# RWKV-7 pair preparation: decay and in-context rate as one 512-wide chain, biases inside the low-rank matmul

## The chip, the cores and the metric

The kernel runs on one core of one Trainium2 chip. The time is device microseconds (us) from launch to end; before the change it is 2669.53 us, the median of three runs (2666.68 to 2670.61). Engines are named as in the profile: PE (TensorE matmul), PEld (its weight loads), DVE (VectorE), ACT (ScalarE), POOL (GpSimd), SP (the queue from which nearly all DMAs are issued).

## The reference

A two-layer trunk on 256 tokens of width 2048. Layer 0 is RWKV-7 time mixing, layer 1 chunked band attention; each is followed by a squared-ReLU MLP, and every sub-layer has an RMS norm with shift, scale and gate computed from a conditioning vector `c`. The change touches only two lines of layer 0, the decay and the in-context rate:

```python
    w_log = -jax.nn.softplus(-(w0 + jnp.tanh(xw @ w1) @ w2)) - 0.5
    a = jax.nn.sigmoid(a0 + (xa @ a1) @ a2)
...
    decay = jnp.exp(-jnp.exp(heads(w_log)))
```

`w1`, `a1` are 2048x96 and `w2`, `a2` are 96x2048; `w0`, `a0` are bias vectors of 2048. Both lines come down to the same thing: with z the biased low-rank product, exp(w_log) is sigmoid(z) times exp(-0.5), and a is sigmoid(z). The kernel gets a sigmoid as exp(-ln(1 + exp(-z))), so that only exponential and logarithm are needed.

## The kernel before, in words

Everything is kept transposed: 128 channels on partitions, 256 tokens along the free axis. Two heads of 64 channels make a *pair*, and layer 0 has 16 pairs.

`layer_a` first computes, for all pairs, the value projection `v` and the low-rank inner products `tw` (96x256, after tanh, line 830), `ta` (96x256, line 831) and `tg`. Then a loop over slots works through the pairs as a software pipeline. Eight slots belong to one pair's dense projections of k and r (`proj_steps`, 2 x 16 contraction tiles, each as three matmuls: lines 407 to 409). A pair itself is a generator of 36 steps, one per slot: 8 of `early` (decay, rate, normalised key, the operands of the chunked recurrence), 12 of `invert` (a triangular inverse in 32x32 tiles), 16 of `late` (the recurrence over four chunks, group norm, gate). Pair j+1 starts 8 slots after pair j, so that four to five pairs are under way at once, each at its own step. In every slot the PE instructions stand in a fixed order (`issue_after`): the inverting pairs first, then the late ones, then the early one, then two portions of the dense projection. From the third pair on, up to six steps per eight slots of the conditioning product (`ada`, line 460 on DVE, fed by 512 KB loads `raw<-w_ada`) go in as filler. On DVE, ACT, POOL and SP no order is written out: when the program is built, a list scheduler with cost estimates lays their instructions into one queue per engine, and on the chip each queue runs strictly in that order.

The steps at issue, all in `Pair.early`:

- step 0: two fp32 matmuls (lines 133, 134) put w and a side by side into one PSUM bank `z`; then for each half DVE adds the bias column and takes the lower bound -80 (line 138, reads PSUM) and ACT takes exp(-z) (line 140).
- step 1: the square of k for the head norm (lines 121 to 125), then on ACT ln(1+x) for each half (line 144), and exp for each half (lines 145, 146).
- step 2: DVE scans the decay along the tokens (line 151), ACT makes its exponentials (lines 153, 155).
- step 3: DVE clamps the head sums out of PSUM (line 160), ACT takes their rsqrt (161 to 163), POOL computes a-1 times `k_a` (165) and a times e2 (167).

Lines 324 to 332, called below the gate of the oldest pair, are the last `late` steps: ln and exp on ACT, three DVE instructions, and the gate matmul (line 330), whose PSUM bank (tag `ms`, two banks) is the one that line 160 of the youngest pair has just read out. The temporaries `s` are 128x256 tiles from one ring of 8 buffers, the oldest free buffer first; a pair takes 14 of them (among them `sw` and `a`). The low-rank weights of a pair, `lw`, are one DMA on SP (line 864) into a single buffer.

Of the kernel before, what the change touches and what calls it, by code (L numbers as in the profile page):

```python
# [12 lines left out]
F32 = mybir.dt.float32  # L13
F32R = mybir.dt.float32r
AF = mybir.ActivationFunctionType
ALU = mybir.AluOpType
AX = mybir.AxisListType

P = 128
# [13 lines left out]

VECS = ["g_mix0", "g_mix1", "g_mlp0", "g_mlp1", "g_kv", "g_final",
        "mu0", "mu1", "mu2", "mu3", "mu4", "mu5",
        "w0", "a0", "k_k", "k_a", "r_k", "ln_w", "ln_b"]
VI = {n: i for i, n in enumerate(VECS)}


# [38 lines left out]
class Pair:  # L78
# [10 lines left out]
        self.b, self.j, self.v, self.tw, self.ta, self.tg, self.e01 = body, j, v, tw, ta, tg, e01  # L89
        self.heads, self.done = (slice(0, C), slice(C, P)), False  # L90

    def s(self, name="s", bufs=8):
        return self.b.pw.tile([P, T], F32, tag=name, bufs=bufs, name=name)

    def big(self, name, bufs):
# [31 lines left out]

    def early(self):
        b, nc, j, k, r, v, s, ch = self.b, self.b.nc, self.j, self.k, self.r, self.v, self.s, self.ch
        pw, vec, cst, e01 = b.pw, b.vec, b.cst, self.e01  # L130
        lw = self.lw
        z = b.psm()
        nc.tensor.matmul(z[:, 0:T], lw[:, 0, :], self.tw, start=True, stop=True)
        nc.tensor.matmul(z[:, T:2 * T], lw[:, 1, :], self.ta, start=True, stop=True)

        sw, a = s(), s()
        for o, at, b0 in ((sw, 0, "w0"), (a, T, "a0")):
            nc.vector.tensor_scalar(out=o, in0=z[:, at:at + T], scalar1=vec(b0, j), scalar2=-80.0,
                                    op0=ALU.add, op1=ALU.max)
            nc.scalar.activation(o, o, AF.Exp, scale=-1.0)  # L140
        yield
        sq = self.parts(k, None, AF.Square, vec("k_k", j))
        for o in (sw, a):
            nc.scalar.activation(o, o, AF.Ln, bias=b.col(C_ONE))
        nc.scalar.activation(sw, sw, AF.Exp, scale=-1.0, bias=b.col(C_MHALF))
        nc.scalar.activation(a, a, AF.Exp, scale=-1.0)
        yield
        pss = b.psm()[:, :T]
        self.head_sums(pss, sq)
        cum = s()  # L150
        nc.vector.tensor_tensor_scan(out=cum, data0=cst("reset"), data1=sw, initial=0.0, op0=ALU.mult, op1=ALU.add)
        e0, e1 = e01[:, :, 0:C], e01[:, :, 1:C + 1]
        nc.scalar.activation(e1, ch(cum), AF.Exp, scale=-1.0)
        e2 = s()
        nc.scalar.activation(e2, cum, AF.Exp)
        self.pc = pw.tile([P, 4, 1], F32, tag="pc", bufs=4, name="pc")
        nc.gpsimd.tensor_copy(self.pc, e01[:, :, C:C + 1])
        yield
        rs, ss, rr = s(), s(), s()
        nc.vector.tensor_scalar(out=ss, in0=pss, scalar1=1e-24, scalar2=None, op0=ALU.max)  # L160
        nc.scalar.activation(rs, ss, AF.Ln)
        nc.scalar.activation(rs, rs, AF.Exp, scale=-0.5)
        nc.scalar.activation(rr, rs, AF.Square)
        km = s()
        nc.gpsimd.tensor_scalar(out=km, in0=a, scalar1=-1.0, scalar2=vec("k_a", j), op0=ALU.add, op1=ALU.mult)
        self.bh, self.kh = s("bh", 2), s("kh", 2)
        nc.gpsimd.tensor_tensor(out=self.bh, in0=a, in1=e2, op=ALU.mult)
        yield
        nc.vector.scalar_tensor_tensor(out=rr, in0=rr, scalar=-0.5, in1=ss, op0=ALU.mult, op1=ALU.mult)
        nc.vector.scalar_tensor_tensor(out=rs, in0=rr, scalar=1.5, in1=rs, op0=ALU.add, op1=ALU.mult)  # L170
        kk = s()
        nc.vector.scalar_tensor_tensor(out=kk, in0=k, scalar=vec("k_k", j), in1=rs, op0=ALU.mult, op1=ALU.mult)
        nc.vector.scalar_tensor_tensor(out=km, in0=km, scalar=1.0, in1=k, op0=ALU.add, op1=ALU.mult)
        yield
        kr = self.kr = self.big("kr", 4)
        nc.vector.tensor_tensor(out=kr[:, :, 0:C], in0=ch(kk), in1=e0, op=ALU.mult)
        nc.vector.tensor_tensor(out=self.bh, in0=self.bh, in1=kk, op=ALU.mult)
        nc.vector.tensor_tensor(out=kr[:, :, C:P], in0=ch(r), in1=e1, op=ALU.mult)
        rkp = s()
        nc.vector.scalar_tensor_tensor(out=rkp, in0=r, scalar=vec("r_k", j), in1=km, op0=ALU.mult, op1=ALU.mult)  # L180
        nc.vector.tensor_tensor(out=self.kh, in0=km, in1=e2, op=ALU.mult)
        rkp = self.parts(rkp, rkp)
        yield

        self.vp = pw.tile([P, 4, C], F32, tag="vp", bufs=4, name="vp")
        pt = b.psm().rearrange("p (a c k) -> p a c k", a=2, c=4)
        self.each(lambda c: pt[:, 0, c, :], lambda c: ch(v)[:, c, :], lambda c: cst("cen"))
        nc.scalar.copy(self.vp, pt[:, 0])
        yield
        pbn = b.psm()[:, :T]  # L190
        self.head_sums(pbn, rkp)
        nc.vector.tensor_tensor(out=v, in0=pbn, in1=v, op=ALU.mult)
        yield
# [142 lines left out]
class Body:  # L336
# [15 lines left out]
    def vec(self, name, kt=None):  # L352
        i = VI[name]
        return self.vecs[:, i, :] if kt is None else self.vecs[:, i, kt:kt + 1]
# [285 lines left out]
    def layer_a(self, st, sp):  # L640
        nc, tc, d = self.nc, self.tc, self.d
        pa = st.enter_context(tc.tile_pool(name="pa", bufs=1))
        v = pa.tile([P, KT, T], F32, name="v")
        tw = pa.tile([96, T], F32, name="tw")
        ta = pa.tile([96, T], F32, name="ta")
        tg = pa.tile([P, 2, T], F32, name="tg")
        with ExitStack() as s1:
            pp = s1.enter_context(tc.tile_pool(name="ps_a", bufs=2, space=bass.MemoryType.PSUM))
# [178 lines left out]
            self.wnext = self.weight(next(weights))  # L827
            for i in range(4):
                nc.scalar.copy(v[:, 2 * i:2 * i + 2, :], pv[i])
            nc.scalar.activation(tw, pl[0][:96, 0, :], AF.Tanh)  # L830
            nc.scalar.copy(ta, pl[0][:96, 1, :])
            ins = nc.scalar.activation(tg, pl[1], AF.Sigmoid)
            with tc.issue_after(ins.ins):
                nc.scalar.preload_act_table_set("natural_log_exp_and_others")
# [4 lines left out]
        with ExitStack() as s1:  # L839
# [14 lines left out]
            def proj_steps(pr):  # L854
                for dst, hl in (("k", xk), ("r", xr)):
# [4 lines left out]
                    for kt in range(KT):  # L860
                        self.proj(ps, w, lambda kt: hl[:, kt, :, 0:T], (kt, kt + 1))
                        if dst == "r" and kt == 1:
                            pr.lw = pw.tile([96, 2, P], F32, tag="lw", bufs=1, name="lw")
                            nc.sync.dma_start(out=pr.lw, in_=d["lora2"][pr.j, :96, 0:2])
                        if kt % 2 == 1:
                            if kt == KT - 1:
                                t = pw.tile([P, T], F32, tag=dst, bufs=2, name=dst)
                                nc.scalar.copy(t, ps)
                                setattr(pr, dst, t)
                            yield  # L870
# [300 lines left out]
def _arrange(x, c, w_ada, b_ada, g_mix, g_mlp, w_up, w_down,  # L1171
# [7 lines left out]
    x, mu = f(x), f(rwkv_mu)[0]  # L1179
    g_mix, g_mlp = f(g_mix), f(g_mlp)  # L1180
    vecs = [g_mix[0], g_mix[1], g_mlp[0], g_mlp[1], f(g_kv), f(g_final)] + [mu[i] for i in range(6)] + [
        f(rwkv_w0)[0], f(rwkv_a0)[0], f(rwkv_k_k)[0], f(rwkv_k_a)[0], f(rwkv_r_k)[0].reshape(D),
        f(rwkv_ln_w)[0], f(rwkv_ln_b)[0]]

    lora1 = np.concatenate([f(w)[0] for w in (rwkv_w1, rwkv_a1, rwkv_g1)], 1)
    lora1 = f(lora1.reshape(4, 4, P, lora1.shape[1]).transpose(0, 2, 1, 3))
    lora2 = np.zeros((NPAIR, P, 4, P), np.float32)
    for i, w in ((0, rwkv_w2), (1, rwkv_a2)):
        w = f(w)[0]
        lora2[:, :w.shape[0], i, :] = w.reshape(w.shape[0], NPAIR, P).transpose(1, 0, 2)  # L1190
    g2 = f(rwkv_g2)[0].reshape(2, P, NPAIR, P)
    lora2[:, :, 2:4, :] = g2.transpose(2, 1, 0, 3)
# [47 lines left out]
```

## Time and profile before

| | |
|---|---|
| runs, median (lowest, highest) | 2669.53 us (2666.68, 2670.61) |
| the profiled execution: its time, its span | 2667.25 us, 2665.3 us |
| HBM read, mean rate | 656.72 MB, 247 GB/s |
| pairs' first low-rank matmul (line 133), first and last | 213.7 us, 626.4 us |

The profiled execution lies within the three runs. A span is the time from the first to the last instruction; the two microseconds between it and the execution's time lie around it. In the views of the profile, `L138 DVE TENSOR_SCALAR s<-ms,vecs` means that line 138 ran on DVE, writing tile `s` from tiles `ms` and `vecs`; behind `x` stands the number of instances, then their busy time in us and the mean of one in ns. `[0.41 <-DVE s L160]` means that the engine sat idle for 0.41 us just before, until line 160 on DVE released it.

### The profile page before, as it was taken

To read this page: it belongs to the slowest core of one execution; us is meant where nothing else is said; L and a number is where in the kernel's file an instruction comes from. 1 tells how busy PE (TensorE), PEld (TensorE's weight loads), DVE (VectorE), ACT (ScalarE), POOL (GpSimd) and SP (SyncE) were. 2 spreads that over 40 slices of the span, in tenths; PEclk is the share of its full clock that TensorE was granted. 3 is DMA by queue.
4 is the path that set the end of the run, shared out by engine and by line. 5 is a ranking of instruction groups with operands and counts; after the bars stand their busy time and mean duration, and the time that the engine had idled before them with its cause. 6 is when DMAs were issued, how large, how long until landed. Compare 5 with 4: busy or idle time off the path is not lost.

```text
span 2665.3 us, 59286 instructions
## 1 busy us (share of the span) xinstructions
PE 2586.9 (97%) x24108; PEld 2258.5 (85%) x24108; DVE 2104.5 (79%) x3070; ACT 1369.2 (51%) x2516; POOL 210.2 (8%) x336
## 2 busy tenths in 40 slices
PE   7998999999999999999999999999999999999997
PEld 4788888888899888888888998877898888888886
DVE  6788888888889888888888898899887556556555
ACT  3345656556456345355365554565564464553554
POOL 0002323223100000000001100000100000000002
PEclk9999999999999999999999999999999999999999
DMA  9976656566768898889888779887766555555553
GB/s 353 313 243 205 202 183 201 182 202 199 252 235 308 309 324 323 318 328 335 319 328 292 231 248 322 320 274 256 267 215 237 185 188 189 184 188 190 189 190 119
DMA packets 207153, 662.69 MB, mean 249 GB/s; under 512 B 21408, under 2 KB 54560, under 8 KB 206880
## 3 DMA queue, kind: packets, MB, share of 16 engines
q1 hardware_dynamic: 204816, 656.36, 71.8%
q8 instruction: 189, 3.10, 0.5%
q10 hardware_dynamic: 2064, 2.54, 0.3%
q14 instruction: 84, 0.69, 0.1%
HBM read 656.72 MB, written 2.10 MB: 247 GB/s over the span
## 4 chain that ended last, share of the span: by engine, by line
PE 83%; DVE 7%; issue 3%; DMA 3%; ACT 2%; POOL 1%; DVEq 0%; ACTq 0%; SPq 0%; POOLq 0%
PE pj L418 41%; PE pj L419 21%; PE pj L407 3%; PE pj L408 3%; PE pj L409 3%; DVE wL L387 2%; DVE acc L460 2%; DMA raw<-w_ada 1%; PE iv L111 1%; DMA rada<-w_ada 1%; ACT wH L384 1%; PE o L407 1%; PE gr L105 1%; PE ms L330 1%; PE o L408 0%
## 5 line engine op out<-in xcount | busy, mean ns | idle before, releaser
L387 DVE TENSOR_TENSOR wL<-raw,wH 128x1024 fp32r<-128x1024 f32 x772 | 941.1, 1220 | 352.8 <-ACT wH L384 346.9
L384 ACT CAST wH<-raw 128x1024 fp32r<-128x1024 f32 x772 | 805.7, 1045 | 783.6 <-PE pj L418 594.6
L418 PE MATMUL pj<-aHL,wH 128*128 128x512 f32 x2816 | 998.1, 398 | 1.3 <-DVE x L953 1.3
L419 PE MATMUL pj<-aHL,wL 128*128 128x256 f32 x2816 | 791.4, 281 | 0.2 <-DVE wL L387 0.2
L418 PE MATMUL pj<-hHL,wH 128*128 128x512 f32 x2048 | 723.0, 398 | 0.0
L418 PEld LDWEIGHTS pj<-aHL,wH 128*128 128x128 f32 x2816 | 531.6, 189 | 129.4 <-issue 8.5
L419 PE MATMUL pj<-hHL,wL 128*128 128x256 f32 x2048 | 573.8, 280 | 0.3 <-DVE wL L387 0.3
L419 PEld LDWEIGHTS pj<-aHL,wL 128*128 128x128 f32 x2816 | 531.6, 189 | 1.8 <-issue 0.8
L418 PEld LDWEIGHTS pj<-hHL,wH 128*128 128x128 f32 x2048 | 384.7, 188 | 95.0 <-DVE hHL L999 0.2
L419 PEld LDWEIGHTS pj<-hHL,wL 128*128 128x128 f32 x2048 | 386.5, 189 | 0.8 <-DVE wL L387 0.6
L460 DVE SCALAR_TENSOR_TENSOR acc<-rada,ct,acc 128x1024 f32<-128x1024 f32 x256 | 328.2, 1282 | 11.1 <-DMA rada<-w_ada 10.1
L407 PE MATMUL pj<-aHL,wH 128*128 128x256 f32 (+1 forms) x896 | 263.3, 294 | 0.1
L408 PE MATMUL pj<-aHL,wH 128*128 128x256 f32 (+1 forms) x896 | 254.7, 284 | 0.0
L409 PE MATMUL pj<-aHL,wL 128*128 128x256 f32 (+1 forms) x896 | 253.5, 283 | 0.0
L524 POOL TENSOR_TENSOR ss<-ss,sq 128x256 f32<-128x256 f32 x56 | 54.1, 966 | 1588.2 <-ACT sq L523 1587.9
L407 PEld LDWEIGHTS pj<-aHL,wH 128*128 128x128 f32 x896 | 170.5, 190 | 5.1 <-issue 0.5
L409 PEld LDWEIGHTS pj<-aHL,wL 128*128 128x128 f32 x896 | 171.0, 191 | 0.2
L408 PEld LDWEIGHTS pj<-aHL,wH 128*128 128x128 f32 x896 | 170.6, 190 | 0.5
L1024 DVE SCALAR_TENSOR_TENSOR x<-pj,mod,x 128x256 f32<-128x256 f32 x256 | 123.4, 482 | 58.5 <-PE pj L419 54.9
L460 DVE SCALAR_TENSOR_TENSOR acc<-raw,ct,acc 128x1024 f32<-128x1024 f32 x104 | 139.9, 1345 | 12.9 <-DMA raw<-w_ada 12.3
L996 ACT ACTIVATE t<-t 128x256 f32<-128x256 f32 x112 | 46.8, 418 | 123.1 <-DVE t L968 123.1
L998 ACT ACTIVATE t<-t 128x256 f32<-128x256 f32 x128 | 53.4, 417 | 3.4
(250 smaller groups left out, 2825.3 us busy)
## 6 DMA issues: line engine op xcount, KB each, us to landing
raw<-w_up SPq DMA_DIRECT2D x256, 512.0 KB, 4.2
raw<-w_down SPq DMA_DIRECT2D x256, 512.0 KB, 4.3
rada<-w_ada SPq DMA_DIRECT2D x209, 512.0 KB, 5.8
raw<-w_ada SPq DMA_DIRECT2D x111, 512.0 KB, 4.4
rada<-w_ada_kv SPq DMA_DIRECT2D x64, 512.0 KB, 6.1
rawa<-w_ada SPq DMA_DIRECT2D x32, 512.0 KB, 6.8
rawa<-w_ada_t SPq DMA_DIRECT2D x32, 512.0 KB, 7.6
raw<-w_k SPq DMA_DIRECT2D x32, 512.0 KB, 3.9
```

The source lines that it names most:

```text
L384: nc.scalar.copy(Hf, raw)
L387: eng.tensor_tensor(out=Lf, in0=raw, in1=Hf, op=ALU.subtract)
L407: nc.tensor.matmul(ps, H[:, i, :], a(kt)[:, 0, :], start=(first and kt == 0), stop=False)
L408: nc.tensor.matmul(ps, H[:, i, :], a(kt)[:, 1, :], start=False, stop=False)
L409: ins = nc.tensor.matmul(ps, L[:, i, :], a(kt)[:, 0, :], start=False, stop=(last and kt == KT - 1))
L418: nc.tensor.matmul(ps, H[:, i, :], a(kt), start=(kt == 0), stop=False)
L419: ins = nc.tensor.matmul(ps[:, 0, :], L[:, i, :], a(kt)[:, 0, :], start=False, stop=(kt == KT - 1))
L460: nc.vector.scalar_tensor_tensor(out=self.acc, in0=raw, scalar=ck, in1=self.acc, op0=ALU.mult, op1=ALU.add)
L524: (eng or nc.gpsimd).tensor_tensor(out=self.ss, in0=self.ss, in1=sq, op=ALU.add)
L996: nc.scalar.activation(t, t, AF.Relu)
L998: nc.scalar.activation(t, t, AF.Square)
L1024: nc.vector.scalar_tensor_tensor(out=x, in0=ps[:, i, :], scalar=self.mods[(layer, 5)][:, n:n + 1], in1=x, op0=ALU.mult, op1=ALU.add)
```

## The change

The biases become row 96 of the low-rank weights, and the rows 96 to 127 of `tw` and `ta` are set to 1 once (rows 97 to 127 of the weights are zero), so that the matmul adds the bias itself. Then both halves of `z` need the same treatment, and lower bound, exponential and logarithm run over all 512 columns in one instruction each. The two last exponentials stay apart (the decay's has the factor exp(-0.5)). The two halves now live in one double-width tile `s2` with one buffer, and the ring `s` goes from 8 buffers to 6. `w0` and `a0` leave the table `vecs`.

```diff
-    def s(self, name="s", bufs=8):
+    def s(self, name="s", bufs=6):
...
-        sw, a = s(), s()
-        for o, at, b0 in ((sw, 0, "w0"), (a, T, "a0")):
-            nc.vector.tensor_scalar(out=o, in0=z[:, at:at + T], scalar1=vec(b0, j), scalar2=-80.0,
-                                    op0=ALU.add, op1=ALU.max)
-            nc.scalar.activation(o, o, AF.Exp, scale=-1.0)
+        both = pw.tile([P, 2 * T], F32, tag="s2", bufs=1, name="s2")
+        sw, a = both[:, 0:T], both[:, T:2 * T]
+        nc.vector.tensor_scalar(out=both, in0=z, scalar1=-80.0, scalar2=None, op0=ALU.max)
+        nc.scalar.activation(both, both, AF.Exp, scale=-1.0)
         yield
         sq = self.parts(k, None, AF.Square, vec("k_k", j))
-        for o in (sw, a):
-            nc.scalar.activation(o, o, AF.Ln, bias=b.col(C_ONE))
+        nc.scalar.activation(both, both, AF.Ln, bias=b.col(C_ONE))
         nc.scalar.activation(sw, sw, AF.Exp, scale=-1.0, bias=b.col(C_MHALF))
         nc.scalar.activation(a, a, AF.Exp, scale=-1.0)
...
-        tw = pa.tile([96, T], F32, name="tw")
-        ta = pa.tile([96, T], F32, name="ta")
+        tw = pa.tile([P, T], F32, name="tw")
+        ta = pa.tile([P, T], F32, name="ta")
+        for t in (tw, ta):
+            nc.gpsimd.memset(t[96:P, :], 1.0)
...
-            nc.scalar.activation(tw, pl[0][:96, 0, :], AF.Tanh)
-            nc.scalar.copy(ta, pl[0][:96, 1, :])
+            nc.scalar.activation(tw[:96, :], pl[0][:96, 0, :], AF.Tanh)
+            nc.scalar.copy(ta[:96, :], pl[0][:96, 1, :])
...
-                            pr.lw = pw.tile([96, 2, P], F32, tag="lw", bufs=1, name="lw")
-                            nc.sync.dma_start(out=pr.lw, in_=d["lora2"][pr.j, :96, 0:2])
+                            pr.lw = pw.tile([P, 2, P], F32, tag="lw", bufs=1, name="lw")
+                            nc.sync.dma_start(out=pr.lw, in_=d["lora2"][pr.j, :, 0:2])
...
-    for i, w in ((0, rwkv_w2), (1, rwkv_a2)):
-        w = f(w)[0]
+    for i, w, bias in ((0, rwkv_w2, rwkv_w0), (1, rwkv_a2, rwkv_a0)):
+        w = np.concatenate([f(w)[0], f(bias)[0].reshape(1, D)], 0)
```

The rest of the diff takes `w0`, `a0` out of the list `VECS` and out of the array that fills it.

More of the change, by code (lines that the diff above doesn't have):

```diff
@@ L35 @@
         "mu0", "mu1", "mu2", "mu3", "mu4", "mu5",
-        "w0", "a0", "k_k", "k_a", "r_k", "ln_w", "ln_b"]
+        "k_k", "k_a", "r_k", "ln_w", "ln_b"]
 VI = {n: i for i, n in enumerate(VECS)}
@@ L1181, in _arrange @@
     vecs = [g_mix[0], g_mix[1], g_mlp[0], g_mlp[1], f(g_kv), f(g_final)] + [mu[i] for i in range(6)] + [
-        f(rwkv_w0)[0], f(rwkv_a0)[0], f(rwkv_k_k)[0], f(rwkv_k_a)[0], f(rwkv_r_k)[0].reshape(D),
+        f(rwkv_k_k)[0], f(rwkv_k_a)[0], f(rwkv_r_k)[0].reshape(D),
         f(rwkv_ln_w)[0], f(rwkv_ln_b)[0]]
```

## The prediction

> **What bounds the kernel now.** First the page, for the busy shares over the whole span.
>
> ```profile
> PE 2586.9 (97%) x24108; PEld 2258.5 (85%) x24108; DVE 2104.5 (79%) x3070; ACT 1369.2 (51%) x2516; POOL 210.2 (8%) x336
> ```
>
> PE is busy nearly throughout. The changed code runs only while pairs are under way, so I took the windows of that stretch (columns: window, its length, busy us of PE, PEld, DVE, ACT, POOL, the granted clock, DMA share, GB/s).
>
> ```profile
> 213.00:640.00 427.00, 403.63 (x8739) 364.89 (x8737) 362.90 (x660) 252.86 (x711) 120.02 (x179) 0.99 0.62 197
> ```
>
> The clock is full. PE is idle for 427.0 - 403.6 = 23.4 us, DVE for 64 us, ACT for 174 us. A shorter instruction on DVE or ACT is worth something only through PE's 23.4 us. So the next view is who PE's weight loads wait for in this window, and each instance of the wait that the early steps can cause.
>
> ```profile
> PEld ms L330 <- DVE s L160: 4.0, 8, 1.4
> ```
>
> ```profile
> 323.89 0.30 PEld L330 LDWEIGHTS ms<-tg,lg 128*128 128x128 f32 x2 [0.20 <-DVE s L160]
> 380.65 0.30 PEld L330 LDWEIGHTS ms<-tg,lg 128*128 128x128 f32 x2 [0.41 <-DVE s L160]
> 409.70 0.30 PEld L330 LDWEIGHTS ms<-tg,lg 128*128 128x128 f32 x2 [1.42 <-DVE s L160]
> 438.05 0.30 PEld L330 LDWEIGHTS ms<-tg,lg 128*128 128x128 f32 x2 [0.20 <-DVE s L160]
> 467.40 0.30 PEld L330 LDWEIGHTS ms<-tg,lg 128*128 128x128 f32 x2 [0.92 <-DVE s L160]
> 495.61 0.30 PEld L330 LDWEIGHTS ms<-tg,lg 128*128 128x128 f32 x2 [0.26 <-DVE s L160]
> 552.39 0.30 PEld L330 LDWEIGHTS ms<-tg,lg 128*128 128x128 f32 x2 [0.20 <-DVE s L160]
> 609.40 0.30 PEld L330 LDWEIGHTS ms<-tg,lg 128*128 128x128 f32 x2 [0.41 <-DVE s L160]
> ```
>
> The gate matmul of an old pair (L330) wants the PSUM bank that L160 of the young pair has not yet emptied. Eight of these waits, 4.0 us. What lies ahead of L160 shows in the chain of waits between 420 and 450 us (start, us, what), for the pair whose matmul is at 438.05:
>
> ```profile
> 430.65 0.80 DVE s L138 x2
> ...
> 431.45 0.71 ACT s L140 x2
> 432.16 0.80 ACT s L144 x2
> ...
> 434.69 0.36 ACT sl L324
> 435.05 0.94 ACT wH L384
> ...
> 436.02 1.22 DVE wL L387
> ...
> 437.66 0.34 DVE s L160
> ```
>
> The first three links are the instructions that the change merges: 0.80 + 0.71 + 0.80 = 2.31 us of a chain that ends in a PE stall. In the pair before, the same wait has another origin (DVE in order of time):
>
> ```profile
> 398.68 0.88 DVE L138 TENSOR_SCALAR s<-ms,vecs 128x256 f32<-128x256 f32 x2
> ...
> 401.03 1.65 DVE L460 SCALAR_TENSOR_TENSOR acc<-raw,ct,acc 128x1024 f32<-128x1024 f32 x1 [1.48 <-DMA raw<-w_ada]
> ...
> 409.23 0.41 DVE L160 TENSOR_SCALAR s<-ms 128x256 f32<-128x256 f32 x1
> ```
>
> ```profile
> 401.00:409.70 8.70, 7.11 (x172) 6.22 (x167) 8.67 (x14) 6.33 (x18) 7.03 (x9) 1.00 0.80 258
> ```
>
> DVE is done with L138, stands 1.48 us for a load, and from 401.03 works without a gap (8.67 of 8.70 us) until L160 releases PE. Anything saved at 398.68 disappears into the 1.48 us.
>
> **The merged instructions.** Widths and engines have rows in the groups by shape, between 213 and 640 us:
>
> ```profile
> L138 DVE TENSOR_SCALAR s<-ms,vecs 128x256 f32<-128x256 f32 x32 | 14.0, 478 | 2.8 <-PE ms L134 2.4
> L160 DVE TENSOR_SCALAR s<-ms 128x256 f32<-128x256 f32 x16 | 6.6, 412 | 0.1
> L219 DVE TENSOR_TENSOR ar<-gr,csts 128x256 f32<-128x256 f32 x15 | 6.3, 418 | 0.0
> L269 DVE TENSOR_TENSOR mk<-gr,csts 128x512 f32<-128x512 f32 x14 | 9.5, 677 | 0.4 <-PE gr L105 0.2
> ...
> L140 ACT ACTIVATE s<-s 128x256 f32<-128x256 f32 x32 | 11.5, 405 | 0.5 <-DVE s L138 0.3
> L144 ACT ACTIVATE s<-s,csts 128x256 f32<-128x256 f32 x32 | 14.4, 495 | 0.0
> L188 ACT COPY vp<-ms 128x256 f32<-128x256 f32 x15 | 5.6, 373 | 6.4 <-PE ms L105 6.4
> L239 ACT COPY bk<-ms 128x512 f32<-128x512 f32 x15 | 8.8, 587 | 0.6 <-PE ms L105 0.2
> ```
>
> L160 is the new DVE form at half the width: a tensor_scalar from PSUM with constants only, 412 ns; the column operand of L138 made it 478. Doubling a PSUM read costs 677 - 418 = 259 ns, so the new one is an estimated 412 + 259 = 671 ns where the chain has 800: 0.13 us saved. On ACT doubling costs 587 - 373 = 214 ns: exp 405 + 214 = 619 ns against 710, 0.09 us saved; ln 495 + 214 = 709 against 800, 0.09 us. Together 0.31 us per pair as links of a chain. If every removed instruction had cost its full mean it would be (956 - 671) + (810 - 619) + (990 - 709) = 757 ns; that is the far end, but two in a row overlap, as their 0.71 us against 2 x 0.405 shows.
>
> [...]
>
> How much of the 0.31 us reaches PE? The two long waits (1.42 and 0.92) save nothing: the first goes back to the load above, and for the second DVE likewise had to stand for a load:
>
> ```profile
> 460.20 2.08 DVE L460 SCALAR_TENSOR_TENSOR acc<-raw,ct,acc 128x1024 f32<-128x1024 f32 x1 [0.15 <-DMA raw<-w_ada]
> ```
>
> The other six are worth the smaller of the wait and 0.31: 0.20 + 0.31 + 0.20 + 0.26 + 0.20 + 0.31 = 1.48 us. That takes all six to hang on this chain, which I saw for the one at 438.05; the end on the other side is 0. The remaining eight pairs have no such wait and give 0: the dense projection's matmuls hide the early steps, and without that cover they would cost at most 0.31 each, 2.5 us more.
>
> **PE.** The matmuls get 128 rows instead of 96. Both forms have rows (ns min/median/max):
>
> ```profile
> L133 PE MATMUL ms<-tw,lw x32: 377/380/483, 213.9 to 626.6; 96*128 96x256 f32 x32
> ...
> L330 PE MATMUL ms<-tg,lg x64: 377/379/484, 323.9 to 709.1; 128*128 128x256 f32 x64
> ```
>
> 380 against 379 ns: rows cost nothing, the bias addition comes free.
>
> **The loads.** `lw` grows from 96 to 128 KB; a 128-partition load of that size is in the table of DMA issues:
>
> ```profile
> lg<-lora SPq DMA_DIRECT2D x16, 128.0 KB, 2.8
> lw<-lora SPq DMA_DIRECT2D x16, 96.0 KB, 3.9
> ```
>
> It is asked for a whole pair ahead and lands in 3 to 4 us, so its own length is hidden. On SP it stays one issue in the same place. But a `w_ada` load behind it can land later by 32 KB at the window's 197 GB/s, 0.17 us; where DVE already stands for that load and PE for DVE, in two pairs, that is 0.3 us. Bounds: 0 and 16 x 0.17 = 2.7 us. I take 0.3.
>
> **The buffers.** A pair now takes 12 tiles from 6 buffers instead of 14 from 8, so a buffer is wanted again after half a pair. By the code at most five of the tiles are alive at once (e2, rs, ss, rr and km in step 3), and the ring hands out the buffer that has been free longest. The new tile `s2` has one buffer; its last reader is L165 on POOL, and the next pair's writer is L138 at 430.65:
>
> ```profile
> 409.01 0.65 POOL L165 TENSOR_SCALAR s<-s,vecs 128x256 f32<-128x256 f32 x1
> ```
>
> 430.65 - 409.66 = 21 us apart. Neither adds a wait that I can see: 0. Were L165 or L138 to wait after all, POOL's and DVE's queues behind it would wait with it, ada's accumulations first; an upper end for that is the rival below. The two memsets stand on POOL ahead of its first work:
>
> ```profile
> 28.39 2.17 POOL L740 TENSOR_TENSOR xx<-h 128x256 f32<-128x256 f32 x2 [27.94 <-DMA rawa<-w_ada_t]
> ```
>
> 27.94 us of idle time cover them; uncovered they would cost about one L165 each, 1.3 us, once. The shorter `vecs` load is worth nothing that a wait shows.
>
> **The sum.** -1.5 + 0.3 = -1.2 us on the profiled execution's 2667.25, 2666.0. That execution is 2.3 us below the median of the runs; the same difference from 2669.5 gives 2668.
>
> **The rivals.** First, the chain is worth its whole length in every pair, because a stage that saves on DVE and ACT lets PE's other idle time shrink too (23.4 us are there). By the rows in order of time the pair of L138 takes 0.88 us, and the merging saves 0.21 instead of 0.13; the ACT rows are
>
> ```profile
> 400.08 0.72 ACT L140 ACTIVATE s<-s 128x256 f32<-128x256 f32 x2
> ...
> 401.11 0.89 ACT L144 ACTIVATE s<-s,csts 128x256 f32<-128x256 f32 x2
> ```
>
> which gives 0.10 and 0.18: 0.49 per pair, 7.8 us in 16, 2662. For it speaks the chain quoted first, which the three merged links lead; against it the pair at 409.70, where a load stood in between. [...]
>
> Second, slower by DVE's order. DVE's queue is laid out anew by estimates at the build. L160 releases PE, and an accumulation takes
>
> ```profile
> L460 DVE SCALAR_TENSOR_TENSOR acc<-raw,ct,acc 128x1024 f32<-128x1024 f32 x84 | 114.5, 1363 | 12.8 <-DMA raw<-w_ada 12.3
> ```
>
> 1.36 us. Where one more of them comes ahead of L160 or of the scan, PE's wait grows like the one of 1.42 us. In eight pairs: 8 x 1.36 - 1.2 = +9.7 us, 2679; it decides from about five pairs on. For it: the new step is shorter, so there is a hole in the list at that place for a filler to fall into. Against it: the estimates change by few tenths of a microsecond per pair.
>
> Third, the change does nothing for PE at all, everything goes into DVE's standing for loads: 2669.5.
>
> **How the numbers follow.** Forecast 2668 (0.30); full chain 2662 (0.28); DVE's order 2679 (0.27); nothing 2669.5 (0.15). About 0.2%, 5.3 us, is what a measurement of this kernel can tell from no change: forecast and third rival lie inside, which makes 0.45; the first is faster (0.28), the second slower (0.27). The range goes from 2661, just beyond the full chain, to 2678, where seven to eight pairs carry the accumulation; the forecast's own is 2667 to 2670.
>
> **What would show it.** One L138 per pair of about 671 ns, one exp of 619, one ln of 709; the first pair of rows says whether the widths were priced well. PE's waits on L160 fall from 4.0 to about 2.5 us, the two long ones stay. L133 at 380 ns. No idle time before L165 or L138 that a buffer explains. The forecast is wrong if PE's busy time plus idle between 213 and 640 us moves by more than 5 us, and the place to look is then what stands between L151 and L160 in DVE's queue.

## The result, and the profile after

| | before | after |
|---|---|---|
| median of nine runs each (lowest, highest) | 2665.91 us (2662.95, 2673.17) | 2659.24 us (2655.02, 2663.75) |
| profiled execution: time, span | 2667.25, 2665.3 | 2658.25, 2656.5 |

The ratio is 0.9975, 95% interval [0.9965, 0.9985]: faster by 0.25%. The 2659.24 us lie below the predicted range of 2661 to 2678 us. The kernel before lies lower too: the forecast started from 2669.53 us, the median of its first three runs, and nine runs give 2665.91. The experiments below change what the 0.25% means: the same two kernels, run again, were equal.

The changed instructions first (groups by shape of the kernel after, 213 to 640 us; behind the bar busy us, then ns of one):

```profile
L142 ACT ACTIVATE s<-s,csts 128x512 f32<-128x512 f32 x16 | 11.6, 722 | 0.5
...
L138 DVE TENSOR_SCALAR s<-ms 128x512 f32<-128x512 f32 x16 | 11.0, 688 | 1.9 <-PE ms L134 1.6
L139 ACT ACTIVATE s<-s 128x512 f32<-128x512 f32 x16 | 10.1, 630 | 4.6 <-DVE s L138 4.5
```

They are within 3% of the estimates of 671, 619 and 709 ns. L133 is unchanged, at 380 ns with 128 rows (min/median/max), and PE's gate matmul, now L328, waits less for the bank that L158 empties: 3.0 us in three waits, where there were 4.0 in eight.

```profile
L133 PE MATMUL ms<-tw,lw x32: 379/380/483, 213.9 to 624.9; 128*128 128x256 f32 x32
```

```profile
PEld ms L328 <- DVE s L158: 3.0, 3, 1.4
```

```profile
436.02 0.73 PEld L328 LDWEIGHTS ms<-tg,lg 128*128 128x128 f32 x4 [0.87 <-DVE s L158]
465.64 0.51 PEld L328 LDWEIGHTS ms<-tg,lg 128*128 128x128 f32 x3 [1.42 <-DVE s L158]
493.24 0.73 PEld L328 LDWEIGHTS ms<-tg,lg 128*128 128x128 f32 x4 [0.70 <-DVE s L158]
```

So the durations came as estimated, and the sum of the waits came near. The single waits did not: the longest one before (1.42 us at 409.70) is gone with four of the six short ones, and the three left have all grown, from 0.20, 0.92 and 0.26 us at the same pairs. Now the time by stage. The stages are cut at the first, third and sixteenth pair's first L133 (ramp, middle), at the 113th cast of a weight half (tail) and at the 129th, where the output projection is nearly over. Before:

```profile
213.90:261.40 47.50, 39.37 (x546) 35.90 (x545) 37.73 (x59) 24.24 (x55) 11.37 (x13) 0.93 0.68 215
261.40:626.30 364.90, 351.68 (x7905) 318.11 (x7903) 311.96 (x575) 216.85 (x623) 100.84 (x156) 1.00 0.61 193
626.30:712.30 86.00, 79.89 (x1561) 70.27 (x1560) 69.78 (x120) 40.37 (x116) 16.31 (x23) 0.98 0.68 224
...
757.50:2665.30 1907.80, 1890.78 (x12265) 1647.30 (x12263) 1484.88 (x1958) 975.67 (x1534) 56.31 (x111) 1.00 0.74 255
```

After:

```profile
213.90:253.30 39.40, 35.96 (x546) 32.98 (x544) 35.94 (x57) 24.27 (x51) 10.61 (x13) 1.00 0.71 237
253.30:624.60 371.30, 353.98 (x7905) 320.19 (x7903) 307.23 (x562) 215.66 (x597) 103.88 (x156) 0.99 0.60 193
624.60:714.60 90.00, 82.06 (x1561) 71.73 (x1560) 69.81 (x119) 39.90 (x113) 15.00 (x23) 0.94 0.66 214
...
759.10:2656.50 1897.40, 1881.24 (x12265) 1643.63 (x12263) 1481.66 (x1959) 975.66 (x1534) 56.55 (x111) 1.00 0.73 257
```

The number of matmuls is the same in each stage. The ramp is 8.1 us shorter, the middle 6.4 longer, the tail 4.0 longer: pairs 498.4 before, 500.7 after. The 10.4 us gained lie behind 757 us, where no changed instruction runs. Two separate questions follow: what moved the pairs by 8 us each way, and what moved the rest.

**The pairs: idle time and clock.** Length minus PE busy is idle: 8.1 to 3.4 us in the ramp, 13.2 to 17.3 in the middle, 6.1 to 7.9 in the tail. That is 4.7 of 8.1, 4.1 of 6.4 and 1.8 of 4.0 us, about half of each shift or somewhat more. The rest is in PE's busy time itself: the same 546 matmuls of the ramp took 39.4 us at a granted clock of 0.93 and 36.0 at 1.00. Slices of 5 us show where the clock went (kernel before):

```profile
225.00:230.00 5.00, 1.94 (x13) 1.54 (x13) 5.00 (x7) 0.62 (x2) 2.27 (x2) 0.98 0.70 234
230.00:235.00 5.00, 5.00 (x35) 4.50 (x35) 2.58 (x5) 1.90 (x5) 0.00 (x0) 0.68 0.60 200
...
250.00:255.00 5.00, 1.26 (x44) 1.22 (x46) 5.00 (x10) 1.27 (x3) 1.81 (x2) 0.86 0.57 202
255.00:260.00 5.00, 5.00 (x72) 4.57 (x68) 3.59 (x6) 0.91 (x3) 0.00 (x0) 0.79 0.61 167
```

Twice PE stands for 3 to 4 us, and twice the clock falls right behind it: (0.02 + 0.32) x 5 = 1.7 us lost, and (0.14 + 0.21) x 5 = 1.75. In the kernel after, all slices from 225 to 260 us have 1.00; its own losses come later, for instance here:

```profile
310.00:315.00 5.00, 3.59 (x90) 3.23 (x87) 4.96 (x10) 4.87 (x11) 4.39 (x6) 1.00 0.72 230
315.00:320.00 5.00, 5.00 (x70) 4.34 (x69) 4.10 (x7) 2.89 (x10) 1.82 (x3) 0.66 0.62 206
```

Cut at the changes of the clock, the two stretches at half speed in the ramp before are each 3.41 us long (229.76 to 233.17 and 253.65 to 257.06 us, granted 0.50), which at half speed is 1.7 us lost; the stretches at full clock behind them last 20.48 and 153.60 us, 6 and 45 times 3.41. In both traces all changes of the clock, from 28 us to the last, lie on such a grid of 3.41 us. In the 3.41 us ahead of 253.65 PE was not busy at all, in those ahead of 229.76 for 0.77 us; but a wholly idle stretch was not needed: ahead of 314.98 us in the kernel after, PE was busy for 2.00 us of 3.41, and the clock fell all the same.

**What PE stood for in the ramp.** PE's waits between 225 and 256 us, before:

```profile
PE iv L111 <- DVE tt L245: 5.0, 2, 4.1
PE ms L116 <- ACT sq L121: 1.6, 1, 1.6
PE ms L116 <- DVE sq L125: 1.5, 1, 1.5
```

The wait of 4.1 us ends with the transpose at 253.29. VectorE's timeline before it (start, us), before:

```profile
247.35 1.28 DVE L460 SCALAR_TENSOR_TENSOR acc<-raw,ct,acc 128x1024 f32<-128x1024 f32 x1 [0.89 <-DMA raw<-w_ada]
...
249.56 0.28 DVE L260 TENSOR_TENSOR u<-u,iv 128x128 f32<-128x128 f32 x1
249.76 0.48 DVE L172 SCALAR_TENSOR_TENSOR s<-k,vecs,s 128x256 f32<-128x256 f32 x1
250.16 0.69 DVE L269 TENSOR_TENSOR mk<-gr,csts 128x512 f32<-128x512 f32 x1
250.76 0.42 DVE L176 TENSOR_TENSOR kr<-s,e 128x256 f32<-128x256 f32 x1
251.09 1.22 DVE L387 TENSOR_TENSOR wL<-raw,wH 128x1024 fp32r<-128x1024 f32 x1
252.22 0.42 DVE L177 TENSOR_TENSOR bh<-bh,s 128x256 f32<-128x256 f32 x1
252.56 0.48 DVE L180 SCALAR_TENSOR_TENSOR s<-r,vecs,s 128x256 f32<-128x256 f32 x1
252.96 0.42 DVE L181 TENSOR_TENSOR kh<-s 128x256 f32<-128x256 f32 x1
253.29 0.31 DVE L245 STREAM_TRANSPOSE tt<-u 128x128 f32<-128x128 f32 x1
```

After:

```profile
244.34 0.28 DVE L258 TENSOR_TENSOR u<-u,iv 128x128 f32<-128x128 f32 x1
244.54 0.42 DVE L174 TENSOR_TENSOR kr<-s,e 128x256 f32<-128x256 f32 x1
244.88 0.42 DVE L175 TENSOR_TENSOR bh<-bh,s 128x256 f32<-128x256 f32 x1
245.21 0.69 DVE L267 TENSOR_TENSOR mk<-gr,csts 128x512 f32<-128x512 f32 x1
245.81 0.53 DVE L179 TENSOR_TENSOR kh<-s 128x256 f32<-128x256 f32 x1
246.26 0.41 DVE L125 TENSOR_TENSOR sq<-s,sq 128x256 fp32r<-128x256 f32 x1
246.60 0.30 DVE L243 STREAM_TRANSPOSE tt<-u 128x128 f32<-128x128 f32 x1
```

PE needs the transpose (L245, L243 after the change) of the sum `u` (L260, L258). Before, a weight half of 1.22 us was among what lay between the two; after, it is not: 3.73 us from the one's start to the other's became 2.26. What lies ahead of the sum changed too. Before, the sum started 2.6 us after PE's matmuls for it had ended (at 246.99), because an accumulation stood for its load and ran in between; after, it started 0.2 us behind them (244.10), and the accumulation stands behind the transpose. PE's wait at this transpose is 0.3 us after the change. The change made nothing of all this shorter; the queue was laid out in another order.

**The middle.** There the order went the other way. An accumulation at the head of VectorE's queue stands until its load has landed (1.48 us at 401.03 in the kernel before), and what is queued behind it stands too (the sum at 249.56 us above). The accumulations' group in the same window, after (before: 12.3 us for the loads, in the prediction):

```profile
L458 DVE SCALAR_TENSOR_TENSOR acc<-raw,ct,acc 128x1024 f32<-128x1024 f32 x84 | 112.9, 1344 | 19.4 <-DMA raw<-w_ada 19.2
```

Compared item by item, the two queues have in eight of pairs 3 to 12 one accumulation more, after, ahead of transposes, sums or subtractions that it stood behind before.

**Behind 757 us: w_down at two paces.** The MLPs' second product (tile `hHL`) runs in eight quarters of 256 weight loads of each kind. The first quarter's `wH` loads (ns min/median/max, first and last start), before:

```profile
L418 PEld LDWEIGHTS pj<-hHL,wH x256: 186/188/188, 867.3 to 958.2; 128*128 128x128 f32 x128
```

After:

```profile
L416 PEld LDWEIGHTS pj<-hHL,wH x256: 186/188/188, 868.9 to 958.1; 128*128 128x128 f32 x128
```

90.9 against 89.2 us for the same instructions, at a median of 357 and 348 ns from one `wH` load to the next. One quarter ran at the fast pace before, seven after. The eight quarters together took 723.0 and 713.6 us: 9.4 of the 10.4 us.

### The profile page after: what moved, and what is told of

It is laid out like the page before. It is cut to its first block, busy times and chain, and to the rows that moved or that the text cites. A ratio compares the mean times of both kernels' runs of the same rounds, so it can differ in the third digit from the quotient of the medians.

```text
span 2656.5 us, 59241 instructions
## 1 busy us (share of the span) xinstructions
PE 2577.0 (97%) x24108; PEld 2253.7 (85%) x24108; DVE 2094.6 (79%) x3054; ACT 1367.6 (51%) x2484; POOL 212.1 (8%) x338
## 4 chain that ended last, share of the span: by engine, by line
PE 81%; DVE 7%; DMA 4%; issue 4%; ACT 2%; POOL 1%; SPq 0%; DVEq 0%; ACTq 0%; POOLq 0%
PE pj L416 42%; PE pj L417 21%; PE pj L405 3%; PE pj L406 3%; PE pj L407 3%; DMA raw<-w_ada 2%; DVE wL L385 2%; DVE acc L458 2%; PE iv L111 1%; PE ms L328 1%; ACT wH L382 1%; DMA raw<-w_o 1%; PE pT L1128 0%; PE o L405 0%; PE m L480 0%
## 5 line engine op out<-in xcount | busy, mean ns | idle before, releaser
L416 PE MATMUL pj<-hHL,wH 128*128 128x512 f32 x2048 | 713.8, 395 | 0.0
L416 PEld LDWEIGHTS pj<-hHL,wH 128*128 128x128 f32 x2048 | 384.1, 188 | 90.1
L458 DVE SCALAR_TENSOR_TENSOR acc<-raw,ct,acc 128x1024 f32<-128x1024 f32 x104 | 138.5, 1331 | 19.4 <-DMA raw<-w_ada 19.2
```

The source lines that it names most:

```text
L416: nc.tensor.matmul(ps, H[:, i, :], a(kt), start=(kt == 0), stop=False)
L458: nc.vector.scalar_tensor_tensor(out=self.acc, in0=raw, scalar=ck, in1=self.acc, op0=ALU.mult, op1=ALU.add)
```

## The experiments

Theories at the start: the queue's order moves the pairs and the pace of w_down falls by chance (order); the shorter instructions themselves save (lengths); smaller `vecs` moves every later tile by 128 bytes, and that sets the pace (address). All edits are small; the stage lengths are cut as above, a quarter counts as fast when its median step is under 352 ns, and ratios are to the kernel before on the same chip.

| run | ratio [95%] | ramp | middle | tail | fast quarters |
|---|---|---|---|---|---|
| before (profile above) | 1 | 47.5 | 364.9 | 86.0 | 1 |
| b_again | 1.0000 [0.9985, 1.0014] | 47.4 | 364.2 | 84.5 | 2 |
| b_low | 1.0008 [0.9998, 1.0017] | 49.0 | 364.9 | 85.9 | 3 |
| after (profile above) | 0.9975 [0.9965, 0.9985] | 39.4 | 371.3 | 90.1 | 7 |
| a_again | 1.0002 [0.9992, 1.0012] | 40.1 | 369.4 | 87.3 | 0 |
| a_again2 | 1.0008 [0.9998, 1.0017] | 40.7 | 370.1 | 88.2 | 0 |
| a_pad | 1.0012 [0.9998, 1.0026] | 41.2 | 368.9 | 89.3 | 0 |
| b_act | 1.0018 [1.0008, 1.0028] | 46.4 | 365.4 | 87.9 | 1 |
| a_max | 0.9989 [0.9979, 0.9999] | 43.9 | 366.6 | 86.4 | 1 |
| a_halves | 0.9989 [0.9978, 1.0000] | 41.0 | 369.6 | 85.5 | 6 |
| b_ramp3 | 1.0002 [0.9990, 1.0014] | 46.0 | 371.3 | 84.6 | 1 |
| b_ramp5 | 0.9989 [0.9978, 1.0000] | 46.2 | 366.5 | 87.0 | 2 |
| a_mid6 | 0.9962 [0.9948, 0.9976] | 39.8 | 364.9 | 89.3 | 4 |
| a_mid5 | 0.9949 [0.9932, 0.9966] | 39.5 | 362.6 | 86.9 | 5 |
| a_mid5_2 | 0.9973 [0.9962, 0.9985] | 39.4 | 362.4 | 84.3 | 0 |
| b_wl | 0.9964 [0.9951, 0.9976] | 38.7 | 366.9 | 84.8 | 2 |
| b_mid5 | 0.9984 [0.9976, 0.9993] | 48.8 | 361.1 | 83.3 | 2 |
| b_both | 0.9962 [0.9948, 0.9975] | 38.8 | 364.2 | 84.2 | 0 |

**The same kernels again, and the addresses.** b_again and a_again are the two kernels unedited. a_pad gives the changed kernel back the old size of `vecs`; b_low takes `w0` and `a0` of the kernel before into a tile of their own on the other side of the memory, so that its later tiles lie 128 bytes lower.

```diff
-        self.vecs = gp.tile([P, len(VECS), KT], F32, name="vecs")
+        vecs_pad = gp.tile([P, len(VECS) + 2, KT], F32, name="vecs")
+        self.vecs = vecs_pad[:, :len(VECS), :]
```

> The kernel before, unchanged, profiled again. In the first two profiles the 8.8 us between the spans stand almost wholly in the w_down matmuls of the two MLPs (L418/L419 on hHL: 7 of 8 quarters at 357 ns a pair of weight loads before, 1 of 8 after; the others 348). Address theory (everything behind the table vecs lies 128 B lower after the change, and the pace follows the address): again 7 of 8 quarters at about 357, ratio 1.000. Chance theory (each quarter falls into one of the two paces in each run, whatever the kernel): another number of slow quarters, anywhere from 1 to 7, ratio 1.000 within its interval. Chain theory (the gain comes from the shorter chain in the pairs): says nothing of the quarters.

> The changed kernel, unchanged, profiled again: ratio 0.9975 in all theories. Address theory: again 7 of 8 quarters at 348 ns. Chance theory: another number. Chain theory: the last pair's L133 again earlier than before, by 1.7 us or more, and the 8 us that the first pairs gain at 240 to 290 us again.

> The changed kernel with the table vecs padded by the two rows that it lost, so that all that lies behind it has the addresses of before; nothing else changes. Address theory: 7 of 8 quarters back at 357 ns, 11 us of the gain lost, ratio to before 0.999 to 1.001. Chance and chain theory: ratio stays 0.9975 (0.9965 to 0.9985).

> The kernel before, with w0 and a0 in a tile of their own at the far end of SBUF, so that everything behind vecs lies 128 B lower, as after the change; the instructions of the pairs are those of before (one small load more). Address theory: most quarters at 348 ns, ratio 0.996 to 0.998 without any merging. Chance and chain theory: ratio 1.000.

The changed kernel came to a ratio of 1.0002, where every theory had expected 0.9975: the 0.25% did not repeat, while the short ramp and the long middle did. Its w_down had no fast quarter where it had had seven; b_low had three, a_pad none. a_pad alone would speak for the address theory, but one and the same program, with its tiles at the same addresses, ran at both paces, and so the theory falls. A chip or a loading of the program that sets the pace is not excluded by this: each of the four groups of runs in this section had a chip of its own, the chip of the first two traces is not on record, and no kernel was traced twice in one group.

**The parts of the change.** b_act is the kernel before with only the exponentials and logarithms merged (and the ring of 6); a_halves is the changed kernel with nothing merged, so that the biases' rows, the larger load and the ring remain of it; a_max has the lower bound merged and nothing else. Of a_halves, the logarithms likewise:

```diff
-        nc.vector.tensor_scalar(out=both, in0=z, scalar1=-80.0, scalar2=None, op0=ALU.max)
-        nc.scalar.activation(both, both, AF.Exp, scale=-1.0)
+        for o, at in ((sw, 0), (a, T)):
+            nc.vector.tensor_scalar(out=o, in0=z[:, at:at + T], scalar1=-80.0, scalar2=None, op0=ALU.max)
+            nc.scalar.activation(o, o, AF.Exp, scale=-1.0)
```

> Kernel before, with the two exponentials and the two logarithms of a pair each made one instruction of 512 elements (ring of 6, one tile of 512 as in the change); the two additions of a bias and lower bound on VectorE stay, and so do the vectors of biases and the 96 rows. In VectorE's queue this leaves pairs 3 to 12 in the order of before, while in pairs 0 and 1 the accumulations and weight halves stand behind the subtractions as in the changed kernel. Order theory: ramp (first to third start of L133's pair) 40 to 42 us as in the changed kernel (before 47.5 to 49), middle (third to sixteenth) 364 to 366 us as before (changed kernel 369 to 371), tail 85 to 87, so some 7 us less than before in the pairs, and a ratio of about 0.9975 beside before if the pace of w_down is alike. Theory of the instructions' own lengths: the ramp is shorter only by what the merged instructions save, under 1 us in two pairs, and the ratio is 0.9995 to 1.0.

> Changed kernel with its biases as rows of the weights and its ring of 6, but with lower bound, exponential and logarithm of each half on its own, 256 elements each, so that no instruction is merged. In VectorE's queue pairs 0 to 12 have the order of the changed kernel. Order theory: ramp 39 to 42, middle 368 to 372, tail 87 to 90 us, as the changed kernel, and a ratio of 0.999 to 1.001 beside before. Theory of the instructions' own lengths: with nothing merged the pattern of before comes back, ramp 47 to 49, middle 364 to 366, tail 84 to 86.

> Changed kernel with only the lower bound merged: exponential and logarithm of each half on their own. In VectorE's queue pair 0 and the first subtraction of pair 1 are as in the kernel with merged exponentials alone, and of pairs 3 to 12 four (4, 6, 8, 10) have an accumulation ahead of work that it stood behind before, against eight in the changed kernel. Order theory: ramp 40 to 43, middle 366 to 369 us, between before and the changed kernel. Theory of lengths: ramp 47 to 49, middle 364 to 366.

> The changed kernel once more, nothing edited. Theory that the pace of w_down falls by chance anew in each run: ratio beside before 0.9975 to 1.001, the fast and slow quarters in another arrangement than in the two profiles so far, and ramp 39 to 42, middle 368 to 372, tail 87 to 90 us again. Theory that the change sets that pace: seven of eight quarters fast and a ratio near 0.9975 again.

a_halves decides between order and lengths. With no instruction merged it has the changed kernel's pattern:

```profile
213.80:254.70 40.90, 37.22 (x545) 34.09 (x544) 35.59 (x59) 24.85 (x55) 9.63 (x13) 0.96 0.71 227
254.70:624.30 369.60, 353.15 (x7905) 319.34 (x7903) 308.43 (x575) 217.19 (x623) 108.57 (x156) 0.99 0.61 194
```

b_act, which has both merges on ACT but in the middle the old order, has the old middle (365.4). Its ramp missed: 46.4 where 40 to 42 was expected, because I had counted as decisive the accumulations ahead of the subtractions L125, and only the waits at L116 fell with those (1.6 and 1.5 us to 1.3 and 0.5); the transposes' waits stayed. Its ratio missed as well (0.9975 expected if the pace were alike). a_halves missed in the tail, 85.5 for 87 to 90. a_max came out in between in the middle (366.6) and missed the ramp by 0.9. a_again2 showed the pattern a third time, again with no fast quarter.

**The order alone.** A tie puts an accumulation behind an earlier-written VectorE instruction in the queue, without a semaphore. b_ramp3 and b_ramp5 tie those of slots 16 to 31 in the kernel before, by three and five slots; a_mid6 and a_mid5 tie those from slot 32 on in the changed kernel, by six and five.

```diff
+                vs.append(self.last_dve())
                 if slot >= 2 * S and slot % 4 < 3:
-                    self.ada()
+                    if slot >= 4 * S:
+                        with tc.issue_after(vs[slot - 5]):
+                            self.ada()
+                    else:
+                        self.ada()
```

> Kernel before with nothing of the change; only the accumulations (L458, L460) that are written in slots 16 to 31 are tied, by order alone and without a semaphore, behind the VectorE instruction that was last three slots earlier. From pair 3 on VectorE's queue is that of before; in pairs 0 to 2 one to two accumulations fewer stand ahead of the subtractions, transposes and sums of the inverse, as in the changed kernel or a little more. Order theory: ramp 40 to 43 us as in the changed kernel (before 47.4 to 49), middle 364 to 366 and tail 84 to 87 us as before, so 5 to 7 us less in the pairs. Theory that the ramp's gain belongs to the change's own instructions: 47 to 49.

> The same tie with five slots in place of three: in pair 0 the subtractions stand where they stood before and only the transposes and sums of the inverse have one accumulation fewer ahead. Order theory: the waits of TensorE for transposes in the ramp (about 5 us before) fall to some 2 to 3 us, its two waits at L116 (1.6 and 1.5 us) stay, ramp 43 to 46 us, middle and tail as before. Theory that the ramp's gain belongs to the change's own instructions: 47 to 49.

> Changed kernel; from slot 32 on each accumulation is tied, by order alone, behind the VectorE instruction that was last six slots earlier. Pairs 0 and 1 keep the changed kernel's queue; in pairs 3 to 12 the queue goes back to within half an accumulation of that of before. Order theory: ramp 39 to 42 us, middle 364 to 367 us (changed kernel 369 to 371), tail 85 to 88, some 5 us less in the pairs than the changed kernel and a ratio of about 0.998 beside before. Theory that the middle's loss belongs to the wider instructions or the larger load: middle 369 to 371.

> The same with five slots: in pairs 3 to 12 the accumulations stand up to one place behind where they stood before at the transposes and sums of the inverse, and one to two behind at the scan. Order theory: middle 362 to 367 us, at or below that of before, unless accumulations that come too late pile up and TensorE waits for them or for the loads they hold up. Theory that the middle's loss belongs to the wider instructions: 369 to 371.

The middle obeyed: 364.9 and 362.6 us for the changed kernel, whose wide instructions and larger load are all still there. a_mid6's tail missed (89.3 for 85 to 88). So the order makes the longer middle. VectorE's standing for the accumulations' loads fell from 19.2 us to 6.2 (a_mid5):

```profile
L458 DVE SCALAR_TENSOR_TENSOR acc<-raw,ct,acc 128x1024 f32<-128x1024 f32 x85 | 112.1, 1318 | 6.6 <-DMA raw<-w_ada 6.2
```

That sum alone does not give the stage's length: it is 13.5 us in a_mid6 (364.9) and 13.7 in a_halves (369.6). PE's waits for the transposes in the middle go along with it better: 3.6 us before, 6.0 after, 8.8 in a_halves, 4.9 and 5.0 with the ties of six and five. Through which waits the order acts is thus shown in part only.

The ramp did not obey: b_ramp3 and b_ramp5 stayed at 46 us, both windows at half clock still there, and the long wait for the transpose with them (3.4 and 3.5 us for 4.1). The timelines above show why: I had moved the accumulations, and between `u` and its transpose the weight half still stood. b_ramp3's middle of 371.3 also missed; that the accumulations held back fell due together in pairs 2 and 3 is a guess.

**The weight halves, and the change against the order.** b_wl writes the halves of the weights of pairs 1 and 2 two slots later in the kernel before. b_mid5 is the kernel before with the tie of a_mid5, b_both has both edits, a_mid5_2 is a_mid5 again.

```diff
-                    self.wnext = None if src is None else self.weight(src)
+                    hold = pr.j in (1, 2) and src is not None
+                    if hold:
+                        raws = [self.raw(src[:, i * HK * P:(i + 1) * HK * P]) for i in range(KT // HK)]
+                    else:
+                        self.wnext = None if src is None else self.weight(src)
...
+                        if hold and kt == 7:
+                            self.wnext = [self.halves(x) for x in raws]
```

> Kernel before with nothing of the change; the halves (cast and subtraction) of the next weights are written two slots later for pairs 1 and 2, the loads where they were. Of VectorE's queue only pairs 0 to 2 differ: the weight half of 1.2 us no longer stands between the sum L260 and the transpose L245 for which TensorE waited 4.1 us in before and 3.4 us where accumulations alone were held back, and pair 0's first subtraction stands ahead of it. Order theory, with the item named that mattered: that wait falls under 2.5 us, the two windows of 3.4 us at half clock near 230 and 254 us (1.7 us lost in each) go or are one fewer, ramp 40 to 44 us (before 47.4 to 49), middle 364 to 367. Theory that the ramp's gain belongs to the change's own instructions: 47 to 49 and both windows stay.

> Kernel before with nothing of the change; from slot 32 on each accumulation is tied, by order alone, behind the VectorE instruction that was last five slots earlier, as in the run of the changed kernel that came to 2653.8 us. Order theory: middle 361 to 364 us (before 364 to 365; changed kernel 369 to 371, with the tie 362.6), ramp 47 to 49 as before, so some 2 us less than before. Theory that the tie only pays together with the change: middle 364 to 367.

> Kernel before with both: the halves of pairs 1 and 2 two slots later, and the tie of five slots from slot 32 on; nothing of the change. Order theory: ramp 40 to 44, middle 361 to 365, tail 84 to 87 us, which is the changed kernel with the tie (39.5, 362.6, 86.9) to within 4 us, so that the change's own instructions are worth under 0.15%. Theory that the change itself is worth several microseconds in the pairs: the sum of the three stays over 494 us.

> The changed kernel with the tie of five slots once more, nothing edited. Order theory: ramp 39 to 42, middle 362 to 364, tail 86 to 88 us again, at most one window at half clock ahead of 600 us; ratio 0.995 to 0.998 beside before, by how many of the eight quarters of w_down fall into the faster pace this time. If the pace were set by this kernel's layout: five quarters fast again and 0.995.

b_wl's VectorE, at the same pair of instructions:

```profile
243.87 0.28 DVE L260 TENSOR_TENSOR u<-u,iv 128x128 f32<-128x128 f32 x1
244.06 0.41 DVE L176 TENSOR_TENSOR kr<-s,e 128x256 f32<-128x256 f32 x1
244.40 0.68 DVE L269 TENSOR_TENSOR mk<-gr,csts 128x512 f32<-128x512 f32 x1
245.00 0.41 DVE L177 TENSOR_TENSOR bh<-bh,s 128x256 f32<-128x256 f32 x1
245.34 0.47 DVE L180 SCALAR_TENSOR_TENSOR s<-r,vecs,s 128x256 f32<-128x256 f32 x1
245.73 0.30 DVE L245 STREAM_TRANSPOSE tt<-u 128x128 f32<-128x128 f32 x1
245.96 1.40 DVE L387 TENSOR_TENSOR wL<-raw,wH 128x1024 fp32r<-128x1024 f32 x1
```

The edit moves all halves of these two pairs, not this one alone. The weight half now follows the transpose, PE's longest wait for a transpose in the ramp is 1.3 us, and the stage has its clock:

```profile
214.10:252.70 38.60, 35.93 (x546) 33.01 (x544) 34.59 (x58) 24.12 (x55) 13.54 (x13) 1.00 0.71 228
```

38.7 us is even under the 40 to 44 expected, with nothing of the change in it (b_both, 38.8, likewise). Again 3.4 us of it is the clock: 35.9 us of busy time where before had 39.4. With both edits the kernel before needs 487.2 us for its pairs, the changed kernel with the tie 489.0 and 486.1: in a like order the change's own instructions are worth nothing that shows. a_mid5_2 missed in the tail, 84.3 for 86 to 88.

The best versions run are the changed kernel with the tie of five slots (2653.83 and 2658.53 us in its two sessions) or of six (2657.23) and the kernel before with the later halves (2656.71) or both edits (2657.08); each beats both kernels of this case as they were run again.

The first `wH` quarter of a_mid5 and then of a_mid5_2, the same program:

```profile
L416 PEld LDWEIGHTS pj<-hHL,wH x256: 186/188/188, 861.0 to 950.2; 128*128 128x128 f32 x128
```

```profile
L416 PEld LDWEIGHTS pj<-hHL,wH x256: 186/188/188, 854.2 to 945.2; 128*128 128x128 f32 x128
```

89.2 and 91.0 us, five fast quarters and none: the pace falls anew for one and the same kernel, here again on another chip.

## Why the prediction was right and wrong

- **Widths, rows and loads: right.** 688, 630 and 722 ns for 671, 619 and 709; L133 at 380 ns.
- **Waits on L160: the total near by luck, the mechanism wrong.** 3.0 us for the predicted 2.5. The merged links were to shorten six short waits and to leave the two long ones. Four of the short ones went, and so did the longest; the other three grew. a_halves, with nothing merged, has 2.0 us in two waits, so the fall does not need the shorter links. The load that was to explain the second long wait (0.92 us) had held DVE for 0.15 us only.
- **"The clock is full": wrong.** I read 0.99 over 427 us and left the clock out. Four windows at half speed stood in the pairs of that run, 1.7 us each, two of them in the ramp; the changed kernel's three traces have two to six (six in the one with the result, three of them in a row from 632.42 us), at other places each time. Slices of 5 us would have shown them, and that PE's waits of 3 to 4 us in the ramp cost about half as much again.
- **"The remaining eight pairs have no such wait and give 0": wrong for pairs 0 to 2.** I looked at the waits on L160 alone. The waits that moved were those for the transposes and subtractions in the ramp, 8.1 us of PE's idle time in 47.5 us.
- **DVE's order: the right rival with the wrong sign and place.** It was priced as accumulations ahead of L160 or of the scan, always a loss. The order did change, by as much as the rival said (8 us), but once for the better (a weight half behind a transpose) and once for the worse (accumulations ahead of transposes in eight pairs), and not mainly at L160. In the profiled pair of runs this nets +2.3 us, and as a mean over two traces of the kernel before and three of the changed one +1.6 (497.3 and 498.9). That the forecast of 1.2 us less is not far from this is luck: two effects of up to 8 us cancel, and it contained neither.
- **The range's lower bound of 2661: the step that failed.** It was set by the full chain, 7.8 us below 2669.5, with two terms put at nothing. One is the starting value: 2669.5 was the median of three runs, and nine runs of the same kernel gave 2665.91. From there the same bound is 2657.4, and 2659.24 lies above it. The other is everything behind the pairs, taken as fixed: the eight quarters of w_down can move by 8 x 1.7 = 13 us without any edit, and in the profile taken with the result they moved by 9.4.
- **The full chain: not what happened.** The measured 6.7 us between the medians look like its 7.8, by coincidence as far as the profile tells: ACT and DVE were busy 2.8 and 6.6 us less between 213 and 640 us, and the pairs got no shorter. The sign named for a wrong forecast could not show this, since busy plus idle time of a fixed window is always its length; cut by stages, the pairs moved by 2.3 us.
- Run again twice, the changed kernel had a ratio of 1.0002 and 1.0008 with intervals that hold 1: nearer to the third rival, nothing, than to the forecast. Over all 30 runs of it the median is 2666.3 us, against 2665.9 for 130 runs of the kernel before. Why all nine runs of the first session lay between 2655 and 2664 is open: only one of them has a trace.

## What to carry to other kernels

Where a queue's order is worked out at the build, changing one instruction can deal the whole queue anew; look at what stands between a producer and its consumer on the critical engine, and fix that order, before pricing nanoseconds of the instructions themselves. Read the granted clock in slices of a few microseconds around PE's longest waits, since a wait of 1.4 to 4 us cost 1.7 us more in clock here. Before believing a quarter of a per cent, run the unedited pair in a second session and compare the stages that no edit touches.

## What the hardware showed that I had not expected

- The clock falls to half for 3.41 us (from 632.42 us in the kernel after for 10.24, three times that; at 28.3 us in both traces for 6.83, twice that) after windows in which PE was idle or only partly busy: 3.59 of 5 us before 315 us in the kernel after. Laid on the grid of 3.41 us that the changes of the clock show, the traces before and after agree between 200 and 715 us: each of the eight falls to half followed a window with at most 2.15 us of busy PE (659.84 to 663.25 us, before), and the least that a window held without one was 1.87 us (656.32 to 659.73 us, after). Executions of one kernel lose it at different places (between 253 and 624 us three windows in the first trace of the changed kernel, at a clock of 0.99 over that stretch; at most one in a_again, at 1.00), so a kernel with waits of this size has an estimated spread of some 1.7 us per such place.
- w_down's identical stream of weight loads and matmuls runs at a median of 348 or 357 ns per step, at a full granted clock in both (1.00 over the first quarter, before and after). In the traces the pace is held over tens of microseconds and changes mostly where PE pauses: the seven changes inside a quarter in the traces before and after came each at a step of 418 to 1184 ns, and in a quarter of b_again it turned fast in the middle, at a step of 1.57 us. In the same quarter of b_wl and b_mid5 it turned fast with no step over 374 ns near that place. What chooses it was not found; the tiles' addresses are excluded by a_mid5 and its repeat, and the change by a_again, while the chip and the loading of the program are open.
